# Hybrid retention and stick-breaking encoder: opening sums, idle products and the engine of the norm statistics

## The chip, the cores and the metric

The kernel runs on one core of a Trainium2 chip. The core has a matrix engine (TensorE, PE in the profile), a vector engine (VectorE, DVE), an engine for activation functions (ScalarE, ACT), a general engine (GpSimd, POOL) and a queue that issues DMA transfers (SyncE, SP). Each engine works off its own instructions in order; semaphores tie the engines together. What counts is the device time of one execution in microseconds (us).

## What is computed

Two layers over a sequence of 1024 frames of 1024 features, in float32. Each layer is one mixer with two head groups:

```python
shift, scale, gate = split(silu(c) @ w_ada + b_ada, 3)
h = rms_norm(x, norm_g) * (1 + scale) + shift
rq, rk, rv, rg, sq, sk, sv, sg = split(h @ w_in)
y_ret = group_norm(retention(rot(rq), rot(rk), rv)) * silu(rg)   # 4 heads x 128
y_sb = stick_breaking(sq, sk, sv) * silu(sg)                     # 8 heads x 64
x = x + gate * (concat(y_ret, y_sb) @ w_out)

def group_norm(o):   # at the end of retention()
    mu = mean(o, -1); var = mean((o - mu) ** 2, -1)
    return (o - mu) * rsqrt(var + 1e-6)
```

A final RMSNorm follows. `shift` and `scale` of the first layer are products of one vector, silu(c), with a 1024 x 2048 part of `w_ada`.

## The kernel before

**Tiling.** Frames and features both come in 8 tiles of 128 (t or b for frames, k for features). Each float32 operand of a large product is split into a float16 part and a float16 remainder (`hh`, `hl` for h; `w[:, 0]`, `w[:, 1]` for weights), and a product is made of three: high x high, high x low, low x high. They write results (`acc`) of 128 x 512 to PSUM. PSUM has eight banks: five for general use (`g`), two for the large results (`pj`), one named `av`, which the opening uses under the name `sums`.

**Order.** `Flow` is a planner that runs while the program is built. Every piece of work is a generator; where it says `yield`, it names what it needs. The planner keeps an estimated clock for each engine, prices each instruction (`price`), and takes the ready piece of the lowest rank; `WARM` is the last rank. The order thus found is fixed in the program. A changed price can so change the order anywhere behind it.

**Opening.** `start` issues, for each k, the loads of two 1024 x 128 parts of `w_ada` (scale and shift, tile `ada`, 512 KB each) and one piece of the first weights (`wst`, split into `w`). Four x tiles come first, four more between k = 1 and k = 2; each x tile is normalised, then transposed on TensorE in two halves (`turned`: 32 transposes each, PSUM tile `xt`) and copied to `xT` (`kept`). With `shift` and `scale` for k known, `kept` makes h: `h32` on GpSimd, `hh` on ScalarE, `hl` on VectorE.

The modulation is a sum over 1024 products for each of 128 columns. Before, for k below 4, `first_direct` makes it on TensorE: 8 products with one result column for scale and 8 for shift, both in float32. For k from 4 on, `first_scale` multiplies and adds on VectorE (8 operations over 128 columns in two running sums and an addition) and `first_shift` multiplies on ScalarE (8) and adds on GpSimd (7); then one product with a column of ones (`first_columns`) adds over the partitions. `summed` reads the column out of the bank `sums` on VectorE. The parts for k = 1, 2, 5 and 6 live in a ring of two buffers: that of k = 5 reuses that of k = 1, and that of k = 6 that of k = 2.

`stick_project` for pair 0 of layer 0 starts while h comes in: `begin` takes all 8 k for four results of the first half, and another `begin` (`later`) for three of the second half. Then the attention of that pair starts with products called `z`.

`awake` fills TensorE with idle products (a constant tile by itself, 256 columns) wherever nothing else is ready, until h for the first half and k = 0 is done.

**Retention.** `retain` treats one block of 128 frames of one head; there are 2 x 4 x 8 = 64. Its result `po` (128 x 128, PSUM, a bank of `g`) goes through `bn_stats` and `bn_aggr` on VectorE (mean and variance), two small operations on GpSimd (variance plus a constant, power -0.5), then `y0` on VectorE, and `yt` on ScalarE and VectorE. The bank goes free when `y0` has been read from it.

Of the kernel before, what the change touches and what calls it, by code (L numbers as in the profile page):

```python
# [13 lines left out]
F32 = mybir.dt.float32  # L14
AF = mybir.ActivationFunctionType
ALU = mybir.AluOpType
# [22 lines left out]
def retention_constants():  # L39
    f = np.float32  # L40
    lg = np.log1p(-(f(2.0) ** (f(-5.0) - np.arange(4, dtype=f)))).astype(f)
    i = np.arange(P, dtype=f)
    m, c = i[:, None], i[None, :]
    same = (i[:, None] // 64) == (i[None, :] // 64)
    later = (c // 64) > (m // 64)
    mask = np.zeros((P, 4, P), f)
    qdec = np.exp((i[:, None] + f(1.0)) * lg[None, :]).astype(np.float64)
    for h in range(4):
        dec = np.exp((np.abs(c - m) - (c + 1)).astype(np.float64) * lg[h])
        mask[:, h] = np.where(same | later, dec * np.exp((m - 127.0) * lg[h]), 0.0) * RS  # L50
    kdec = np.exp((f(127.0) - i)[:, None] * lg[None, :]).astype(f)
    bdec = [float(np.exp(f(P) * lg[h])) for h in range(4)]


    cols = np.concatenate([kdec * f(DS * VS), EPS * P * (VS * RS / qdec) ** 2], 1).astype(f)
    return mask, cols, bdec
# [43 lines left out]
class Flow:  # L100
# [32 lines left out]
    def price(self, kind, name, outs, ins):  # L133
# [12 lines left out]
        if kind == "act":  # L146
            scales = sum(1 for a in ins[1:] if a.free_size() == 1)
            return n / 1.2 + (51 if ins[0].space == PSUM else 93) + 93 * scales
# [144 lines left out]
def trunk(ctx: ExitStack, tc, x, c, norm_g, w_ada, b_ada, w_in, w_out, final_g,  # L293
# [195 lines left out]
    def first_scale(ks, scale):  # L489

        yield (), roomt.has()
        roomt.n -= 1
        two = f2("acc").rearrange("p (a f) -> p a f", a=2)[:, :, 0:len(ks) * P]
        for r in range(NK):
            yield [scale], None, "dve"
            acc = two[:, r % 2]
            if r < 2:
                dve.tensor_scalar(acc, scale[:, r], c_act[:, r:r + 1], None, op0=ALU.mult)
            else:
                dve.scalar_tensor_tensor(out=acc, in0=scale[:, r], scalar=c_act[:, r:r + 1], in1=acc,  # L500
                                         op0=ALU.mult, op1=ALU.add)
        acc = two[:, 0]
        dve.tensor_add(acc, acc, two[:, 1])
        yield [acc]
        yield from first_columns(acc, ks, 1)
        roomt.n += 1
# [460 lines left out]
    def retain(l, h, b, acc, state, turn, mask):  # L967
# [17 lines left out]
        dve.scalar_tensor_tensor(out=gs, in0=acc[:, 384:512], scalar=DS, in1=gs,  # L985
# [19 lines left out]

        old, old16 = state[0] or (None, None)
        if b < NT - 1:
# [18 lines left out]
            state[0] = new, new16  # L1026
        yield [("qkT", l, h, b)], roomg.has(), "pe"
# [15 lines left out]
        if b > 0:  # L1043
# [3 lines left out]
        st = wk.tile([P, 6], F32, tag="rbs", name="rbs")  # L1047
        dve.bn_stats(out=st, in_=po[:, 0:P])
        mv = wk.tile([P, 2], F32, tag="rmv", name="rmv")
        dve.bn_aggr(out=mv, in_=st)  # L1050
        ve = wk.tile([P, 1], F32, tag="rve", name="rve")
        pool.tensor_tensor(out=ve, in0=mv[:, 1:2], in1=rcols_sb[:, 4 + h:5 + h], op=ALU.add)
# [3 lines left out]
        dve.scalar_tensor_tensor(out=y0, in0=po[:, 0:P], scalar=mv[:, 0:1], in1=gs,  # L1056
                                 op0=ALU.subtract, op1=ALU.mult)
# [217 lines left out]
    def start():  # L1275
# [34 lines left out]
        for k in range(NK):  # L1310
# [13 lines left out]
            for i, third in enumerate((1, 0)):  # L1324
# [5 lines left out]
                f = first_direct([k], st, third) if k < 4 else (first_shift, first_scale)[third]([k], st)  # L1330
# [12 lines left out]
    def awake():  # L1343

        idle = bank("idle", "pj", 2)
        while True:
            yield [own]
            if ("h", 0, 0, 0) in flow.done:
                return
            pe.matmul(idle[:, 0:256], own[:, 0:P], own[:, 0:256], start=True, stop=True)  # L1350
# [28 lines left out]
```

## Time and profile before

| | |
|---|---|
| runs of before | 1087.74, 1092.58, 1222.69 us, median 1092.58 |
| profiled execution | 1092.43 us, span 1090.0 us |
| TensorE busy | 1053.6 us (97%) |
| VectorE busy | 879.2 us (81%) |
| ScalarE busy | 550.7 us (51%) |
| GpSimd busy | 247.7 us (23%) |
| read from HBM | 92.32 MB |

The span is the time from the first to the last instruction in the trace; 2.4 us lie outside it. In the rows further down, a row of the windows gives the stretch, its length, the busy time of PE, its weight loads (PEld), DVE, ACT and POOL with the number of instructions, the granted TensorE clock as a share of 2.4 GHz, the busy share of the DMA engines and what they moved in GB/s. A row of the timeline gives start, duration, engine, line, operation, result and operands, shapes, count, and in brackets the idle time before it and what ended it. The line is L90 nearly everywhere, that of the recording helper, so the names of tiles tell the work apart. A row of waits gives who waited for whom: total, times, longest. Float32 products appear as two records each where the result has one column. Matmul records overlap, since they are pipelined; the distance between starts is what one costs.

### The profile page before, as it was taken

To read this page: it belongs to the slowest core of one execution; us is meant where nothing else is said; L and a number is where in the kernel's file an instruction comes from. 1 tells how busy PE (TensorE), PEld (TensorE's weight loads), DVE (VectorE), ACT (ScalarE), POOL (GpSimd) and SP (SyncE) were. 2 spreads that over 40 slices of the span, in tenths; PEclk is the share of its full clock that TensorE was granted. 3 is DMA by queue.
4 is the path that set the end of the run, shared out by engine and by line. 5 is a ranking of instruction groups with operands and counts; after the bars stand their busy time and mean duration, and the time that the engine had idled before them with its cause. 6 is when DMAs were issued, how large, how long until landed. Compare 5 with 4: busy or idle time off the path is not lost. (4 is left out here: it accounts for less than half of the span.)

```text
span 1090.0 us, 18647 instructions
## 1 busy us (share of the span) xinstructions
PE 1053.6 (97%) x6472; PEld 525.4 (48%) x6472; DVE 879.2 (81%) x1673; ACT 550.7 (51%) x1263; POOL 247.7 (23%) x557
## 2 busy tenths in 40 slices
PE   6989999999999999999899999999999999999996
PEld 5834444444455544544445444444454445545443
DVE  2488998899899968999455788976899789999544
ACT  3566556535454455481444555544645555555112
POOL 2382330133014202320100034000133013343002
PEclk8699999999999999999999999999999999999999
DMA  9915756766686746367581565665735473647664
GB/s 291 241 50 137 157 112 150 181 137 162 156 201 150 155 91 143 69 172 180 171 239 61 120 142 104 138 159 120 158 78 139 85 153 71 150 82 175 198 238 144
DMA packets 343901, 159.61 MB, mean 146 GB/s; under 512 B 228032, under 2 KB 319232, under 8 KB 343808
## 3 DMA queue, kind: packets, MB, share of 16 engines
q1 hardware_dynamic: 343808, 158.44, 60.3%
q8 instruction: 50, 0.82, 0.3%
q14 instruction: 43, 0.35, 0.1%
HBM read 92.32 MB, written 11.53 MB: 95 GB/s over the span
## 5 line engine op out<-in xcount | busy, mean ns | idle before, releaser
L90 PE MATMUL acc<-hh,w 128*128 128x512 f16 x1024 | 323.0, 381 | 0.7 <-DVE q L90 0.6
L90 PE MATMUL acc<-w,hh 128*128 128x512 f16 x1024 | 305.0, 379 | 0.0
L90 PEld LDWEIGHTS <-w 128*128 128x128 f16 x1536 | 145.7, 99 | 179.7 <-issue 21.3
L90 PE MATMUL acc<-hl,w 128*128 128x512 f16 x512 | 195.0, 381 | 0.8 <-DVE hl L90 0.8
L90 PE MATMUL acc<-w,hl 128*128 128x512 f16 x512 | 194.0, 379 | 0.0
L90 POOL TENSOR_TENSOR t<-t,t 128x128 f32<-128x128 f32 (+1 forms) x192 | 130.9, 696 | 232.6 <-DVE t L90 196.4
L90 PE MATMUL acc<-w,y 128*128 128x512 f16 (+1 forms) x792 | 170.8, 374 | 3.3 <-ACT y L90 3.1
L90 PEld LDWEIGHTS <-hh 128*128 128x128 f16 x1024 | 92.3, 98 | 96.8 <-issue 10.8
L90 DVE TENSOR_TENSOR_SCAN keep<-keep,own 128x640 f32<-128x640 f32 (+3 forms) x60 | 114.3, 1911 | 18.8 <-ACT keep L90 18.7
L90 PEld LDWEIGHTS <-y 128*128 128x128 f16 x792 | 76.5, 98 | 91.2 <-ACT y L90 3.6
L90 DVE SCALAR_TENSOR_TENSOR w<-wst,w 128x512 f16<-128x512 f32 x160 | 110.8, 714 | 8.2 <-ACT w L90 7.9
L90 ACT ACTIVATE w<-wst 128x512 f16<-128x512 f32 x160 | 96.5, 635 | 15.2 <-DMA wst<-in_w_in_dram 11.9
L90 ACT CAST t<-t 128x256 f16<-128x256 f32 (+1 forms) x128 | 44.3, 352 | 88.5 <-POOL t L90 53.3
L90 ACT CAST keep<-beta 128x640 f16<-128x640 f32 (+3 forms) x60 | 53.0, 885 | 63.5 <-DVE beta L90 63.2
L90 PEld LDWEIGHTS <-hl 128*128 128x128 f16 x512 | 50.1, 98 | 60.4
L90 ACT ACTIVATE keep<-z 128x512 f32<-128x512 f32 (+3 forms) x120 | 63.7, 531 | 20.6 <-PE z L90 20.1
L90 DVE TENSOR_TENSOR keep<-beta,keep 128x640 f16<-128x640 f32 (+3 forms) x60 | 61.2, 1024 | 7.5 <-ACT keep L90 7.5
L90 PE MATMUL z<-k,q 64*128 64x512 f16 (+3 forms) x576 | 64.6, 328 | 1.3 <-ACT beta L90 0.5
L90 ACT ACTIVATE beta<-z 128x512 f32<-128x512 f32 (+4 forms) x120 | 64.3, 536 | 0.0
L90 DVE SCALAR_TENSOR_TENSOR beta<-beta,keep 128x639 f32<-128x639 f32 (+3 forms) x60 | 62.5, 1047 | 0.0
L90 DVE TENSOR_TENSOR t<-acc,turn 128x256 f32<-128x256 f32 x128 | 47.9, 415 | 17.2 <-ACT vd L90 16.2
L90 DVE TENSOR_TENSOR_SCAN both<-both,own 128x128 f32<-128x128 f32 (+3 forms) x64 | 55.1, 869 | 7.2 <-ACT both L90 7.2
(122 smaller groups left out, 1307.4 us busy)
## 6 DMA issues: line engine op xcount, KB each, us to landing
wst<-in_w_in_dram SPq DMA_DIRECT2D x128, 256.0 KB, 3.5
wst<-in_w_ada_dram SPq DMA_DIRECT2D x64, 256.0 KB, 3.1
ada<-in_w_ada_dram SPq DMA_DIRECT2D x16, 512.0 KB, 6.5
wst<-in_w_out_dram SPq DMA_DIRECT2D x32, 256.0 KB, 3.4
x<-xh SPq DMA_DIRECT2D x24, 256.0 KB, 2.6
xt<-in_x_dram SPq DMA_DIRECT2D x8, 512.0 KB, 5.3
turn<-in_rot_dram SPq DMA_DIRECT2D x64, 64.0 KB, 2.3
xt<-x SPq DMA_DIRECT2D x8, 512.0 KB, 4.4
```

The source lines that it names most:

```text
L90: real(*args, **kw)
```

## The change

It has four parts.

1. In the opening, `first_direct` now serves k = 0 and 1 for both parts, and k = 2, 3 and 5 for shift alone. `first_scale` serves k = 2 to 7, and `first_shift` k = 4, 6 and 7.
2. `first_scale` is four VectorE operations on the loaded tile: one multiplication over 1024 columns, with silu(c) spread over 128 columns each, and three additions of 512, 256 and 128 columns.
3. Idle products run until h for the second half and k = 7 is planned, and they write columns 256 to 511 of the bank `sums` instead of a tile of their own in `pj`.
4. In `retain`, the statistics come from ScalarE: one activation copies `po` and gives the negative mean by its accumulator, a second squares `po` minus the mean and gives the sum of squares. The constants are scaled to match, `y0` adds the negative mean, and a mark orders the states of successive blocks. The planner's price for an activation with two results rises by 186 ns.

```diff
     def first_scale(ks, scale):
-        yield (), roomt.has()
-        roomt.n -= 1
-        two = f2("acc").rearrange("p (a f) -> p a f", a=2)[:, :, 0:len(ks) * P]
-        for r in range(NK):
+        yield [scale], None, "dve"
+        dve.tensor_tensor(out=scale, in0=scale, in1=c_act[:, :, None].broadcast_to([P, NK, P]), op=ALU.mult)
+        for n in (4, 2, 1):
             yield [scale], None, "dve"
-            acc = two[:, r % 2]
-            if r < 2:
-                dve.tensor_scalar(acc, scale[:, r], c_act[:, r:r + 1], None, op0=ALU.mult)
-            else:
-                dve.scalar_tensor_tensor(out=acc, in0=scale[:, r], scalar=c_act[:, r:r + 1], in1=acc,
-                                         op0=ALU.mult, op1=ALU.add)
-        acc = two[:, 0]
-        dve.tensor_add(acc, acc, two[:, 1])
-        yield [acc]
-        yield from first_columns(acc, ks, 1)
-        roomt.n += 1
+            dve.tensor_add(scale[:, 0:n], scale[:, 0:n], scale[:, n:2 * n])
+        yield [scale]
+        yield from first_columns(scale[:, 0], ks, 1)
...
+        if b > 0:
+            yield [("state", l, h, b - 1)]
...
         yield [po]
-        st = wk.tile([P, 6], F32, tag="rbs", name="rbs")
-        dve.bn_stats(out=st, in_=po[:, 0:P])
-        mv = wk.tile([P, 2], F32, tag="rmv", name="rmv")
-        dve.bn_aggr(out=mv, in_=st)
+
+        junk = turned[:, P:]
+        nm = wk.tile([P, 1], F32, tag="rmv", name="rmv")
+        act.activation(junk, po[:, 0:P], AF.Identity, scale=-1.0 / P, accum_out=nm)
+        yield [nm]
+        sq = wk.tile([P, 1], F32, tag="rbs", name="rbs")
+        act.activation(junk, po[:, 0:P], AF.Square, bias=nm[:, 0:1], accum_out=sq)
+        yield [sq]
         ve = wk.tile([P, 1], F32, tag="rve", name="rve")
-        pool.tensor_tensor(out=ve, in0=mv[:, 1:2], in1=rcols_sb[:, 4 + h:5 + h], op=ALU.add)
+        pool.tensor_tensor(out=ve, in0=sq, in1=rcols_sb[:, 4 + h:5 + h], op=ALU.add)
...
-                f = first_direct([k], st, third) if k < 4 else (first_shift, first_scale)[third]([k], st)
+                f = first_direct([k], st, third) if k < 2 or (k in (2, 3, 5) and not third) else (first_shift, first_scale)[third]([k], st)
...
-        idle = bank("idle", "pj", 2)
+        idle = sums[:, 256:512]
         while True:
             yield [own]
-            if ("h", 0, 0, 0) in flow.done:
+            if ("h", 0, 1, 7) in flow.done:
                 return
-            pe.matmul(idle[:, 0:256], own[:, 0:P], own[:, 0:256], start=True, stop=True)
+            pe.matmul(idle, own[:, 0:P], own[:, 0:256], start=True, stop=True)
```

Over the whole program TensorE has 62 idle products instead of 39, 56 direct sums instead of 64 and 9 column sums instead of 8. All other products are the same in number.

On TensorE, in the opening, `xt` is the transpose of the second half of x, `sums<-c_act,ada` a direct sum and `acc<-hh,w` a product of `begin`. Before, this is how the sums for k = 3 stand:

```order
L90 LDWEIGHTS w
L90 MATMUL acc<-hh,w 128x512
L90 MATMUL sums<-c_act,ada 128x1 x16
L90 MATMUL xt<-ident,xt 128x128 x32
L90 LDWEIGHTS w
L90 MATMUL acc<-hh,w 128x512
```

Now the place between the first products and the transposes reads so (tile numbers shown; of the idle products `sums<-own`, 13 stand ahead of the direct sums of shift 2 and four behind them; `ada_280` holds the parts for k = 2):

```order
L90 LDWEIGHTS own_76
L90 MATMUL sums_113<-own_76 128x256
L90 MATMUL sums_113<-c_act_100,ada_280 128x1 [waits DMAHW3_49]
L90 MATMUL sums_113<-c_act_100,ada_280 128x1 x7
...
L90 MATMUL sums_113<-own_76 128x256 [waits DVE_49]
L90 LDWEIGHTS w_127 [waits Activation_49]
...
L90 MATMUL xt_477<-ident_71,xt_278 128x128
L90 MATMUL sums_113<-c_act_100,ada_288 128x1 [waits DMAHW6_49]
L90 MATMUL sums_113<-c_act_100,ada_288 128x1 x7
```

The direct sums for k = 3 (`ada_288`, shift alone) moved from ahead of the transposes to behind them, those of scale 2 and 3 are gone from here, and an idle product waits for VectorE.

On VectorE, in the opening, before, the sum for scale 5 and what stands among it (`s` and `sh` are the finished columns):

```order
L90 TENSOR_SCALAR acc<-ada,c_act 128x128
L90 TENSOR_TENSOR s_111<-sums,bg 128x1
L90 TENSOR_TENSOR s_111<-s_111,bg 128x1
L90 TENSOR_SCALAR acc<-ada,c_act 128x128
L90 SCALAR_TENSOR_TENSOR acc<-ada,c_act,acc 128x128 x4
L90 TENSOR_TENSOR sh_109<-sums,bg 128x1
L90 SCALAR_TENSOR_TENSOR acc<-ada,c_act,acc 128x128 x2
L90 TENSOR_TENSOR acc<-acc 128x128
```

Now, the place where scale 2 ends and scales 3 and 4 start:

```order
L90 TENSOR_TENSOR hl<-h_460,hh 128x512
L90 COPY xT<-xt 128x512
L90 SCALAR_TENSOR_TENSOR w<-wst,w 128x512
L90 TENSOR_TENSOR ada<-ada 128x128
L90 SCALAR_TENSOR_TENSOR w<-wst,w 128x512
L90 TENSOR_TENSOR sh_109<-sums,bg 128x1
L90 TENSOR_TENSOR ada<-ada,c_act 128x1024
L90 TENSOR_TENSOR s_111<-sums,bg 128x1
L90 TENSOR_TENSOR s_111<-s_111,bg 128x1
L90 SCALAR_TENSOR_TENSOR w<-wst,w 128x512
L90 TENSOR_TENSOR ada<-ada 128x512
L90 TENSOR_TENSOR ada<-ada,c_act 128x1024
```

The eight operations on 128 columns became one on 1024 and three additions, and the end of scale 2 moved behind the copies of the transposed second half.

## Rows read from the trace of the kernel before

**Rows 1.** Windows: busy time in the two long stretches behind the opening

```profile
120.00:540.00 420.00, 411.00 (x2631) 199.76 (x2630) 371.49 (x707) 218.85 (x514) 90.86 (x217) 1.00 0.65 149
540.00:1000.00 460.00, 455.44 (x2827) 218.63 (x2825) 382.06 (x730) 244.22 (x573) 98.63 (x228) 1.00 0.55 126
```

**Rows 2.** Waits of PE over the whole span, longest first

```profile
PE acc L90 <- ACT y L90: 3.1, 2, 1.6
PE sums L90 <- POOL ada L90: 2.8, 2, 1.5
...
PE acc L90 <- DVE hl L90: 0.8, 1, 0.8
PE sums L90 <- DVE acc L90: 0.7, 1, 0.7
...
PE sums L90 <- DVE sh L90: 0.4, 1, 0.4
```

**Rows 3.** Timeline of PE: the opening, and transposes of layer 1 at 540 us

```profile
9.13 6.89 PE L90 MATMUL idle<-own 128*128 128x256 bf16 x37
...
26.93 3.73 PE L90 MATMUL sums<-c_act,ada 128*128 128x1 f32 x32 [0.41 <-DVE sh L90]
...
34.46 3.96 PE L90 MATMUL sums<-c_act,ada 128*128 128x1 f32 x32
...
40.56 6.82 PE L90 MATMUL sums<-c_act,ada 128*128 128x1 f32 x32
47.24 6.10 PE L90 MATMUL xt<-ident,xt 128*128 128x128 f32 x32
53.18 0.38 PE L90 MATMUL acc<-hh,w 128*128 128x512 f16 x1
...
92.25 0.36 PE L90 MATMUL z<-k,q 64*128 64x128 f16 x6
...
540.19 0.60 PE L90 MATMUL pht<-ident,xt 128*128 128x128 f32 x4
540.62 2.75 PE L90 MATMUL acc<-w,y 128*128 128x512 f16 x12
```

**Rows 4.** Chain that ended last: start, us, what; a stretch of dense products

```profile
1006.91 24.61 PE acc L90 x114
```

**Rows 5.** Windows of the opening: granted clock (third number from the end) and transfers

```profile
26.93:30.50 3.57, 3.57 (x32) 3.57 (x33) 2.86 (x6) 3.15 (x6) 1.98 (x4) 1.00 1.08 287
...
40.56:47.20 6.64, 6.64 (x33) 6.64 (x32) 0.28 (x1) 0.21 (x1) 0.00 (x0) 0.50 1.18 291
47.24:53.10 5.86, 5.86 (x33) 5.86 (x34) 3.29 (x6) 3.78 (x7) 2.66 (x3) 0.58 0.46 130
...
53.18:92.25 39.07, 34.78 (x169) 16.14 (x167) 31.91 (x74) 23.88 (x56) 27.05 (x44) 1.00 0.12 35
```

**Rows 6.** Timeline of ACT: the last normalisation of an x tile

```profile
39.63 1.14 ACT L90 ACTIVATE xt<-xt,rs 128x1024 f32<-128x1024 f32 x1
```

**Rows 7.** Timeline of the DMA queue: the pair of loads for k = 6

```profile
38.69 2.60 SPq L90 DMA_DIRECT2D ada<-in_w_ada_dram  x2
```

**Rows 8.** Groups by line and form: VectorE operations near the new ones

```profile
L90 DVE TENSOR_TENSOR keep<-beta,keep 128x1024 f16<-128x1024 f32 x16 | 19.5, 1216 | 2.5 <-ACT keep L90 2.5
...
L90 DVE TENSOR_TENSOR xh<-xh,up 128x512 f32<-128x512 f32 x24 | 16.6, 692 | 1.6 <-DMA xh<-x 0.9
...
L90 DVE SCALAR_TENSOR_TENSOR acc<-ada,c_act,acc 128x128 f32<-128x128 f32 x24 | 9.9, 465 | 0.0
```

**Rows 9.** Groups by line and form: the statistics on DVE, and nearest ACT rows

```profile
L90 DVE BATCH_NORM_STATS2 rbs<-po 128x6 f32<-128x128 f32 x64 | 18.3, 287 | 3.3 <-PE po L90 3.1
...
L90 DVE BATCH_NORM_AGGREGATE rmv<-rbs 128x2 f32<-128x6 f32 x64 | 11.6, 182 | 2.2
...
L90 ACT ACTIVATE rg<-acc 128x128 f32<-128x128 f32 x64 | 17.6, 275 | 28.6 <-PE acc L90 28.6
...
L90 ACT ACTIVATION_READ_ACCUMULATOR junk<-xt 128x1 f32 x22 | 4.1, 187 | 0.0
```

More of the change, by code (lines that the diff above doesn't have):

```diff
@@ L52, in retention_constants @@
     bdec = [float(np.exp(f(P) * lg[h])) for h in range(4)]
-    cols = np.concatenate([kdec * f(DS * VS), EPS * P * (VS * RS / qdec) ** 2], 1).astype(f)
+    cols = np.concatenate([kdec * f(DS * VS), EPS * P * P * (VS * RS / qdec) ** 2], 1).astype(f)
     return mask, cols, bdec
@@ L147, in price @@
             scales = sum(1 for a in ins[1:] if a.free_size() == 1)
-            return n / 1.2 + (51 if ins[0].space == PSUM else 93) + 93 * scales
+            read = 186 * (len(outs) > 1)
+            return n / 1.2 + (51 if ins[0].space == PSUM else 93) + 93 * scales + read
         if kind == "dve":
@@ L984, in retain @@
                                  op0=ALU.mult, op1=ALU.subtract)
-        dve.scalar_tensor_tensor(out=gs, in0=acc[:, 384:512], scalar=DS, in1=gs,
+        dve.scalar_tensor_tensor(out=gs, in0=acc[:, 384:512], scalar=DS * P ** 0.5, in1=gs,
                                  op0=ALU.mult, op1=ALU.mult)
@@ L1026, in retain @@
             state[0] = new, new16
+            flow.mark(("state", l, h, b))
         yield [("qkT", l, h, b)], roomg.has(), "pe"
@@ L1055, in retain @@
         y0 = sm
-        dve.scalar_tensor_tensor(out=y0, in0=po[:, 0:P], scalar=mv[:, 0:1], in1=gs,
-                                 op0=ALU.subtract, op1=ALU.mult)
+        dve.scalar_tensor_tensor(out=y0, in0=po[:, 0:P], scalar=nm[:, 0:1], in1=gs,
+                                 op0=ALU.add, op1=ALU.mult)
         roomg.n += 1
```

## The prediction

> **What bounds the kernel now.** I read the windows of busy time first. Behind the opening TensorE hardly rests: 411.0 of 420 us between 120 and 540 us, 455.4 of 460 between 540 and 1000 [rows 1]. So past the opening an edit is worth at most the 13.6 us of rest in the first two windows, and only where a wait of TensorE hangs on it. The longest of those waits are for `y` from ScalarE, 3.1 us in two pieces [rows 2].
>
> The opening is different: TensorE is "busy" there with work that is small or of no use. The timeline [rows 3] shows, in order: 37 idle products, direct sums of the modulation (16 for each k, 32 records), at 47.24 us the 32 transposes of the second half of x, and from 53.18 us the product stream of `begin`. That stream is the first work of any size: 8 k x 7 results x 3 = 168 products of 512 columns. The program's order puts 12 ahead of the sums for k = 2 and 6 behind them, so 150 remain at 53.18 us. One costs 24.61 / 114 = 0.216 us [rows 4], so 150 cost 32.4 us; TensorE waits 2.8 + 0.8 + 0.7 = 4.3 us for modulation and `hl` [rows 2]; that leaves, of the 39.1 us to the first product for `z` at 92.25 us [rows 3], 2.4 us for eight column sums: 0.3 each.
>
> The reader should look at one place above all: the sums for k = 3 fill 40.56 to 47.24 us, 6.82 us for a job that took 3.73 us at 26.93 us. The granted clock tells why: 1.00 in the early stretch, 0.50 in the late one, that is the lower level of 1.2 GHz, not the upper of 2.4 [rows 5]. The transposes queue behind them, although their last input was normalised at 39.63 + 1.14 = 40.8 us [rows 6], and run at a mean of 0.58 themselves [rows 5]. Everything after 92 us is a full TensorE, so a microsecond won before it should arrive at the end.
>
> **The opening, step by step.** The order of TensorE is common to both kernels up to 34.46 us (one idle product fewer). From there the changed order has 13 idle products, the 8 sums of shift 2, 4 idle products, 3 products for k = 1, then the transposes. Idle products cost 6.89 / 37 = 0.186 us with the clock up [rows 3]; 13 cost 2.4 us, twice that at the lower level. I take 2.9, because the clock was low just before and I expect it to rise during them. Eight sums are half of 3.73 or half of 6.82 us: 1.9 to 3.4, and I take 1.9, since idle products stand ahead. Four idle products are 0.7 us, and the last of them waits for VectorE, which reads a sum from the same bank: 0.4 us, by the one such wait of before, for `sh` [rows 2]. Three products are 0.65. So the transposes can start at 34.46 + 2.9 + 1.9 + 1.1 + 0.65 = 41.0 us. Their input is there: in ScalarE's order the last normalisation, which ended at 40.8 us [rows 6], no longer stands behind the `hh` of k = 2 and its wait for a sum.
>
> The transposes take 5.9 us at the lower level (47.24 to 53.18); at full clock four take 0.43 us (540.19 to 540.62 [rows 3]), so 32 take 3.5. I take 5.0, because two engines that also have `hl` and `hh` to make copy the results out of three banks. The dense stream then starts at 46.0 us instead of 53.18. Bounds: everything at the upper level, 43.7; everything at the lower, 50.9.
>
> Behind it TensorE has more to do than before: 153 products (33.0 us), 16 direct sums that were moved behind the transposes (shift 3 and shift 5, 3.7 us), nine column sums at 0.3 us (2.7), seven idle products (1.3). That is 40.7 us. Of the 4.3 us of waits I leave 1.0. The sums of VectorE are shorter: for one k, eight operations at about 0.47 us and an addition, some 4.2 us, become one pass of 1024 (1.22 us, by the nearest row) and additions of 512, 256 and 128 (0.69, then 0.42 and 0.30 as an estimate on the line through these two rows): 2.6 us [rows 8]. In 53 to 92 us VectorE was busy 31.9 us, GpSimd 27.1, ScalarE 23.9 [rows 5]. With 5 scales of 2.6 for 4 of 4.2 VectorE has 28, and GpSimd loses the seven additions of shift 5. All fit under 40.7 us of TensorE work, which is the cover; without it the chain of sum, `h` and `hl` shows again, with 4.3 us as before. So `z` begins at 46.0 + 40.7 + 1.0 = 87.7 us, **4.6 us earlier**. By the bounds: 43.7 + 40.7 + 0 = 84.4 (7.9 earlier) and 50.9 + 40.7 + 4.3 = 95.9 (3.6 later).
>
> **A transfer that gets later.** The pair for k = 6 reuses the buffer of k = 2. Before, it was issued at 38.69 us [rows 7]; now it must wait for the column sum of scale 2, which the new order puts six products and eight sums behind the transposes, at about 46.0 + 1.9 + 1.3 = 49.2 us. Behind it in SP's queue stand a weight piece, the pair for k = 7 and another piece: 2.5 MB, about 9 us at 291 GB/s [rows 5], so to some 59 us. The products for k = 7 are the last 21 before `z`, from about 87.7 - 21 x 0.216 = 83.2 us, and the chain from landing to them (2.6 us of sums, `h`, `hl`) is a few us. I charge nothing; it would cost only if the pair slipped by some 15 us more.
>
> **The norm statistics.** On VectorE two operations of 0.287 and 0.182 us go, 64 times: 30.0 us [rows 9]. On ScalarE two activations and two reads of the accumulator come, 2 x (0.275 + 0.187) = 0.92 us [rows 9], 59 us in all, on an engine that was busy 218.9 of 420 and 244.2 of 460 us [rows 1]; the second activation waits for the first's sum, with the sigmoids of the attention queued behind it and VectorE's scans behind those. The chain from `po` to the statistics is 0.45 us longer. In no row of before does TensorE wait for these statistics [rows 2]; what hides them is the products of other heads. A relieved VectorE can shorten the 3.1 us of `y`, a fuller ScalarE can lengthen them. Bounds: 3 us gained, or 64 x 0.45 = 29 us lost if every block passed its delay on through a bank that `po` holds. I take 0.5 gained.
>
> **Sum.** 1092.43 (the profiled execution, span 1090.0; the median of 1092.58 is next to it) - 4.6 - 0.5 = 1087.3, say **1087**.
>
> One rule speaks against the idle products. The wait on TensorE for VectorE's read of a sum is 0.4 us, once [rows 2]. The Trainium skill, "PSUM — Partial Sum Buffer", section "PSUM bank collisions raise a hardware error", says that two engines must not touch one bank in the same partitions at once, even at different columns, so it is to be guarded bank by bank; the idle products now share the bank of the sums. By it each of the three groups of idle products behind 34 us waits for a read, 1.2 us at the row's price in place of the 0.4 in the sum: 1088.1 instead of 1087.3. No row of before has idle products in that bank, so none can say which.
>
> **Rivals.** (a) *The clock stays up.* If the idle products hold the upper level through sums and transposes, the early bounds hold: 7.9 us from the opening, and with the 3.1 us of `y` waits 1092.4 - 11.0 = **1081**. For it: the clock was 1.00 right after the first transposes; against: it was 0.50 through 6.6 us of sums [rows 5], and sums remain. The Trainium skill, "TensorE: Matmul & The Clock Gate", Part 1, says that the throttled level is the default and activity releases it; by that rule this case would be the likely one, and the trace agrees in the direction alone. (b) *The gain is lost again*, because the transposes start no earlier (copies, a low clock) or because the order behind 92 us, newly made by the planner, has 5 us more of waits beside its 13.6: **1092**. For it: the planner's order behind 92 us differs in many places. Against: TensorE's work there is the same, piece for piece. (c) *ScalarE becomes the bound of the retention chain.* `po` holds one of five banks until VectorE has the mean, and the mean now waits in ScalarE's queue behind sigmoids. If half the 64 blocks pass 0.45 us on, that is +14: 1092.4 - 4.6 + 14 = **1102**; it decides from about 12 blocks on (12 x 0.45 = 5.4, more than the 5.1 gained). Against: ScalarE is idle half the time.
>
> **How the numbers follow.** My forecast (1084 to 1091) 0.50, (a) 0.17, (b) 0.20, (c) 0.13. From 1080 to 1095 holds the forecast, (b) and most of (a): the range. Faster by over 2% would need 1070.7, beyond every bound but a sum of all: 0.01. Slower by over 2% (above 1114; 2% is about what a measurement here can tell from no change) needs (c) at nearly full price: 0.04. The rest, 0.95, is no difference.
>
> **What would show it.** Right: transposes at 40 to 42 us, stream from about 46, `z` at 86 to 89; nearly no waits between; a thinner stretch of DMA around 43 to 49 us; the clock not at 0.50 for 12 us on end. Wrong: transposes at 45 or later; `z` past 91; TensorE waiting for `po`'s banks or ScalarE; more than 17 us of rest between 120 and 1000 us.

## The result and the profile after

The changed kernel takes 1101.93 us (median; 1097.51 to 1106.59), the kernel before 1089.32 in the same comparison. The ratio is 1.0120, 95% interval [1.0091, 1.0150]: 1.2% slower, outside the predicted 1080 to 1095. The profiled execution took 1106.59 us with a span of 1104.8. The run of before at 1222.69 us counts in its median, but is left out of the ratio as a slow run.

The engine busy times moved as the diff says: VectorE 851.1 us (879.2 before), ScalarE 591.6 (550.7), GpSimd 281.7 (247.7). TensorE is busy 1056.0 of 1104.8 us, 2.4 us more than before.

The timeline of TensorE in the opening answers [rows 3]: columns are start, duration, engine, line, operation, operands, shapes, count, and the idle time ahead with what ended it.

```profile
37.32 2.92 PE L90 MATMUL xt<-ident,xt 128*128 128x128 f32 x24
40.93 1.21 PE L90 MATMUL xt<-ident,xt 128*128 128x128 f32 x8 [0.69 <-ACT xT L90]
41.98 2.15 PE L90 MATMUL sums<-c_act,ada 128*128 128x1 f32 x16
43.98 0.59 PE L90 MATMUL acc<-hh,w 128*128 128x512 f16 x1
...
77.62 1.01 PE L90 MATMUL sums<-ones,ada 128*128 128x1 f32 x4 [2.27 <-DVE ada L90]
...
92.46 0.45 PE L90 MATMUL z<-k,q 64*128 64x128 f16 x7
```

The transposes start 10 us earlier than the 47.24 us of before and the dense stream 9 us earlier than 53.18; yet the first product for `z` comes at 92.46 us, where before had 92.25. The nine microseconds are gone by 92 us. How many of the nine were the program's own is taken up further down, with a second execution of each kernel. Here is the window from the dense stream to `z`, to be held against the last of [rows 5], in which before was busy for 34.78 of 39.07 us:

```profile
43.98:92.46 48.48, 44.51 (x196) 20.98 (x197) 35.23 (x63) 23.11 (x48) 30.61 (x39) 0.87 0.35 90
```

TensorE idles 4.0 us there, no more than the 4.3 of before, but it is busy 9.7 us longer. One part of this is the work that the change moves behind the transposes, by the forecast's count 40.7 us for 34.8. The other part is the clock. These are windows of after (granted clock third from the end):

```profile
44.00:46.00 2.00, 2.00 (x6) 0.70 (x7) 1.35 (x3) 1.27 (x4) 1.38 (x2) 0.50 0.04 8
...
58.00:60.00 2.00, 2.00 (x6) 0.76 (x5) 1.41 (x3) 2.00 (x8) 1.92 (x3) 0.50 0.97 273
...
78.00:84.00 6.00, 6.00 (x17) 2.42 (x17) 2.20 (x6) 2.04 (x3) 2.20 (x8) 0.50 0.00 0
```

These ten microseconds ran at 1.2 GHz; at the upper level the same work would have taken about 5 us less, as an estimate. SP's queue, which answers [rows 7], and ScalarE's timeline show what else is late:

```profile
46.95 1.26 SPq L90 DMA_DIRECT2D ada<-in_w_ada_dram  x2
48.29 1.25 SPq L90 DMA_DIRECT2D wst<-in_w_in_dram  x1
```

```profile
56.07 0.63 ACT L90 ACTIVATE w<-wst 128x512 f16<-128x512 f32 x1 [5.81 <-DMA wst<-in_w_in_dram]
```

The pair for k = 6 is issued at 46.95 us (before: 38.69), and the weight piece behind it at 48.29. ScalarE, in its order, waits 5.81 us for that piece; the `hh` of k = 3 and the products of the next shift sums stand behind the wait. Since TensorE's own idle time is no longer than before, this wait is not shown to cost it anything.

The larger loss is behind `z`. From the first product for `z` to the end of the span I call *the remainder*: 1104.8 - 92.46 = 1012.3 us, against 1090.0 - 92.25 = 997.8 before, **14.6 us more**. The windows that answer [rows 1], from `z` on (length, then TensorE's busy time), and the row that sums them:

```profile
92.46:540.00 447.54, 433.31 (x2751) 208.58 (x2750) 375.65 (x688) 254.41 (x684) 110.45 (x224) 1.00 0.68 150
540.00:1000.00 460.00, 450.52 (x2787) 216.32 (x2786) 363.47 (x655) 261.67 (x676) 105.13 (x220) 1.00 0.55 123
1000.00:1104.80 104.80, 94.61 (x525) 46.95 (x522) 55.74 (x86) 27.74 (x70) 20.92 (x34) 0.98 0.66 187
sum 1012.34, PE 978.43 PEld 471.85 DVE 794.87 ACT 543.82 POOL 236.50; mean PE 326.14 PEld 157.28 DVE 264.95 ACT 181.27 POOL 78.83
```

The same three windows of before sum to this:

```profile
sum 997.75, PE 974.92 PEld 471.08 DVE 829.07 ACT 502.29 POOL 205.52; mean PE 324.98 PEld 157.03 DVE 276.36 ACT 167.43 POOL 68.51
```

TensorE idles 1012.34 - 978.43 = 33.9 us in after and 22.8 in before. So 11.1 of the 14.6 us are new idle time and 3.5 are longer busy time, which was not traced. The waits of TensorE behind `z` (total, times, longest), beside [rows 2], name the first new one. The first row is from after, the second from before:

```profile
PE psc L90 <- POOL t L90: 9.4, 10, 2.1
```

```profile
PE psc L90 <- POOL t L90: 1.3, 5, 0.5
```

`psc`, the first product of a retention block, waits 9.4 us for the rotated tile `t` from GpSimd; before, that wait was 1.3 us. On GpSimd stand the two small operations behind the statistics, `rve` and `rrs`. In the groups by form (total, mean ns of one) they last 0.50 and 0.96 us, where before had 0.190 and 0.652 (after first, then before):

```profile
L90 POOL TENSOR_TENSOR rrs<-rve,nhalf 128x1 f32<-128x1 f32 x64 | 61.3, 958 | 5.0
...
L90 POOL TENSOR_TENSOR rve<-rbs,rcols_sb 128x1 f32<-128x1 f32 x64 | 31.7, 495 | 91.2 <-ACT t L90 91.1
```

```profile
L90 POOL TENSOR_TENSOR rrs<-rve,nhalf 128x1 f32<-128x1 f32 x64 | 41.7, 652 | 5.0
...
L90 POOL TENSOR_TENSOR rve<-rmv,rcols_sb 128x1 f32<-128x1 f32 x64 | 12.1, 190 | 123.2 <-DVE rmv L90 119.5 <-ACT keep L90 3.6
```

The prices that [rows 8] and [rows 9] stood for came out as follows: the scale of one k takes 1.306 + 0.724 + 0.527 + 0.584 = 3.14 us, not 2.6; the statistics take 0.280 + 0.205 + 0.372 + 0.203 = 1.06 us a block on ScalarE, not 0.92. The additions of the scale sums are not dearer by themselves. At their shortest the three take 0.68, 0.42 and 0.28 us, as forecast. Of the six over 128 columns, the first had no GpSimd operation beside it and took 0.28 us; the other five had one, and took 0.47 to 0.77 us. Here are the mean, the first and the last of them:

```profile
L90 DVE TENSOR_TENSOR ada<-ada 128x128 f32<-128x128 f32 x6 | 3.5, 584 | 0.0
```

```profile
43.15 0.28 DVE L90 TENSOR_TENSOR ada<-ada 128x128 f32<-128x128 f32 x1
...
76.80 0.77 DVE L90 TENSOR_TENSOR ada<-ada 128x128 f32<-128x128 f32 x1
```

### The profile page after: what moved, and what is told of

Read it like the earlier page. It is cut to its first block, busy times and chain, and to the rows that moved or that the text cites. A ratio compares the mean times of both kernels' runs of the same rounds, so it can differ in the third digit from the quotient of the medians.

```text
span 1104.8 us, 18789 instructions
## 1 busy us (share of the span) xinstructions
PE 1056.0 (96%) x6481; PEld 520.6 (47%) x6481; DVE 851.1 (77%) x1533; ACT 591.6 (54%) x1511; POOL 281.7 (26%) x550
## 4 chain that ended last, share of the span: by engine, by line
PE 37%; DVE 6%; issue 4%; POOL 4%; DMA 2%; ACT 2%; SPq 2%; POOLq 0%; DVEq 0%; ACTq 0%
PE acc L90 31%; PE z L90 2%; PE av L90 2%; SPq L90 2%; POOL t L90 1%; DMA xt<-x 1%; DVE t L90 1%; POOL rrs L90 1%; DVE keep L90 1%; PE po L90 1%; DVE beta L90 1%; POOL rve L90 1%; PE psc L90 1%; DVE w L90 1%; DVE h L90 1%
## 5 line engine op out<-in xcount | busy, mean ns | idle before, releaser
L90 PE MATMUL acc<-hh,w 128*128 128x512 f16 x1024 | 327.2, 386 | 1.4 <-DVE q L90 1.2
L90 PE MATMUL acc<-hl,w 128*128 128x512 f16 x512 | 197.7, 386 | 0.0
L90 POOL TENSOR_TENSOR t<-t,t 128x128 f32<-128x128 f32 (+1 forms) x192 | 123.3, 656 | 280.4 <-DVE t L90 233.5
L90 ACT ACTIVATE keep<-z 128x512 f32<-128x512 f32 (+3 forms) x120 | 63.5, 529 | 14.6 <-PE z L90 14.0
L90 POOL TENSOR_TENSOR rrs<-rve,nhalf 128x1 f32<-128x1 f32 x64 | 61.3, 958 | 5.0
```

Source lines behind the costliest of these rows:

```text
L90: real(*args, **kw)
```

## The experiments

The questions were which part makes the remainder longer, whether the parts work by themselves or through the planner's order, and what the opening really gained. All figures stand in one table; the edits and what they showed follow. "Remainder" is span minus start of `z`, of the profiled execution; "idle t" is TensorE's wait for `t` from GpSimd behind `z`; the pair is the mean of `rve` and `rrs` in ns.

| kernel | `z` at | remainder | idle t | pair | time, us | ratio to before |
|---|---|---|---|---|---|---|
| before | 92.25 | 997.8 | 1.3 | 190, 652 | 1089.3 | |
| before again (g4) | 86.33 | 997.4 | 1.6 | 192, 652 | 1085.87 (one run) | |
| changed | 92.46 | 1012.3 | 9.4 | 495, 958 | 1101.93 | 1.0120 [1.0091, 1.0150] |
| changed again (f4) | 88.54 | 1012.2 | 9.9 | 500, 967 | 1102.5 (one run) | |
| e1 opening alone | 87.10 | 1005.4 | 3.2 | 189, 648 | 1098.11 | 1.0114 [1.0057, 1.0171] |
| e2 statistics alone | 87.99 | 1006.4 | 8.5 | 455, 914 | 1096.42 | 1.0079 [1.0051, 1.0107] |
| e3 idle products alone | 88.63 | 1006.1 | 2.3 | 197, 670 | 1096.91 | 1.0080 [1.0048, 1.0111] |
| e4 before, planner's margin 410 | 96.20 | 1004.1 | 1.9 | 203, 672 | 1096.82 | 1.0060 [1.0028, 1.0093] |
| f2 before, margin 390 | 87.56 | 1007.7 | 4.6 | 189, 646 | 1100.94 | 1.0095 [1.0064, 1.0126] |
| f1 statistics on ScalarE, order of before | 86.19 | 1001.6 | 2.8 | 293, 736 | 1097.33 | 1.0052 [1.0018, 1.0086] |
| f3 changed, margin 410 | 91.36 | 1008.8 | 8.9 | 553, 906 | 1102.76 | 1.0112 [1.0055, 1.0170] |
| g1 statistics on VectorE, changed order | 88.76 | 1012.4 | 7.5 | 456, 859 | 1103.62 | 1.0149 [1.0090, 1.0208] |
| g2 changed, GpSimd priced as measured | 91.31 | 1007.2 | 5.7 | 467, 837 | 1100.31 | 1.0109 [1.0063, 1.0154] |
| g3 changed, scale 2 on TensorE | 94.79 | 1008.2 | 9.2 | 488, 775 | 1103.87 | 1.0149 [1.0101, 1.0197] |
| h1 as g1, `y0` moved up | 91.74 | 1025.6 | 9.4 | 262, 914 | 1118.31 | 1.0265 [1.0227, 1.0303] |

**Each part alone, and the planner alone (e1 to e4).** The variants of before also carry the mark on the states of successive blocks (the `yield [("state", ...)]` and `flow.mark` of the diff); alone, it leaves the order of every engine as it was, as f1 further down shows, which carries it too. e1 has parts 1, 2 and 3 of the change (`first_scale`, the line that chooses between the three kinds of sum, and the idle products), e2 part 4 with its price of 186 ns; their edits stand in the diff ahead. e3 has part 3 alone, and e4 none of them; no run has parts 1 and 2 without part 3:

```diff
# e3
-        idle = bank("idle", "pj", 2)
+        idle = sums[:, 256:512]
-            if ("h", 0, 0, 0) in flow.done:
+            if ("h", 0, 1, 7) in flow.done:
-            pe.matmul(idle[:, 0:256], own[:, 0:P], own[:, 0:256], start=True, stop=True)
+            pe.matmul(idle, own[:, 0:P], own[:, 0:256], start=True, stop=True)
# e4
-SLACK = 400
+SLACK = 410
```

`SLACK` is the margin in ns that the planner adds when TensorE must wait for another engine. It is in no instruction; it only makes another order.

> The changed kernel with the norm statistics put back on VectorE (bn_stats, bn_aggr); the opening's edits and the mark on the states stay. In the trace of the changed kernel the first product for z starts at 92.5 us against 92.25 before, and the 12 us are lost behind it. Theory A (the statistics on ScalarE cost the 12 us, the opening nothing): within 3 us of before, z at 91 to 94 us. Rival B (any new order of the planner behind the opening costs this): 1096 to 1103, as changed. Rival C (the opening costs it, by leaving work late for what follows): 1099 or more.

> The kernel before with only the statistics moved to ScalarE (and the planner's price of 186 ns for it). Theory A: 1099 to 1103, 10 to 13 us above before; GpSimd's two small operations behind the statistics take 0.4 us or more and 0.8 us or more in the mean instead of 0.19 and 0.65, and TensorE waits 6 us or more for the rotated t. Rival C: 1087 to 1091. Rival B: anything between 1085 and 1103, with no tie to the waits for t.

> The kernel before with only the idle products changed: longer, and in the bank of the sums. If the idle products alone keep the clock up and let the transposes start earlier, z at 88 to 91 us and 1085 to 1088. If the sums for k = 3 still stand in front of the transposes, nothing changes: z at 91 to 93 us, within 2 us of before. Rival B: a new order, up to 10 us above before.

> The kernel before with one constant of the planner changed (SLACK 410 instead of 400 ns): the same instructions in another order on every engine from about the first z on. Theory A: within 3 us of before. Rival B (the order alone moves the time by as much as the change did): 5 us or more away from before, either side.

All four are slower, and their remainders lie between 1004.1 and 1006.4 us. e1, e3 and e4 came out as rival B has it. e2 has the long pair and the waits for `t` of theory A (8.5 us), but takes 1096.4 us, less than its 1099 to 1103. The one that changes nothing but the planner's margin loses 6.3 us behind `z`, where those with real parts lose 7.6 to 8.6. So a part's price can't be read from a kernel in which the planner has ordered everything anew.

**The order held or varied (f1 to f4).** f1 takes before with its order held: the planner is told of `bn_stats` and `bn_aggr`, and the program gets the two activations at that place. f2 is before with a margin of 390 and f3 the changed kernel with one of 410, each by the one line shown for e4; f4 is the changed kernel once more.

```diff
# f1
-        dve.bn_stats(out=st, in_=po[:, 0:P])
-        dve.bn_aggr(out=mv, in_=st)
+        act.real.activation(junk, po[:, 0:P], AF.Identity, scale=-1.0 / P, accum_out=nm)
+        act.real.activation(junk, po[:, 0:P], AF.Square, bias=nm, accum_out=sq)
+        flow.note("dve", "bn_stats", [st], [po[:, 0:P]])
+        flow.note("dve", "bn_aggr", [mv], [st])
```

> The kernel before with the statistics on ScalarE, but with the planner told that they are still bn_stats and bn_aggr on VectorE: TensorE, GpSimd and the DMA queue keep the order of before instruction by instruction. If moving the statistics itself costs (the GpSimd pair behind them gets slower and the rotated t comes late): 1095 to 1100, with the pair above 0.4 and 0.8 us in the mean and the rest of the program behind z 5 us or more longer than the 997.8 us of before. If only the new order cost (theory B): 1086 to 1091, the rest of the program 996 to 1000 us.

> The kernel before with the planner's constant SLACK at 390 instead of 400 ns, a second order without any other edit. If the order of before is one of the good ones among many (theory B): 1092 to 1100, the rest behind z 1002 to 1008 us, as in the run with 410. If 410 was a bad draw: within 3 us of before.

> The changed kernel with SLACK at 410: the same edits, another order. Theory B alone: the rest behind z falls to 1003 to 1008 us, where the other orders of the kernel before lie. If the statistics on ScalarE cost on top of it: 1008 to 1014 again, with 6 us or more of waits of TensorE for t.

> The changed kernel once more, for a second trace of its opening. In the run with the opening's edits alone z began at 87.1 us, in the changed kernel's first trace at 92.5 after a wait of 2.3 us and a fall of the clock to 0.50 around 80 us. If that was the draw of one execution: z at 86 to 90 us here. If it belongs to the program: 91 to 94.

In f1's trace every engine has the order of before, apart from the exchanged operations. In that order ScalarE's statistics cost 1001.6 - 997.8 = 3.8 us in the remainder; that, and the pair at 293 and 736 ns, lies between the two cases expected. The margin of 390 costs 9.9 us, with nothing changed in the work. Here are the sums of the windows behind `z` for the two orders of before that are new by the margin alone, 410 (e4) and 390 (f2):

```profile
sum 1004.10, PE 975.97 PEld 473.06 DVE 825.42 ACT 500.78 POOL 199.70; mean PE 325.32 PEld 157.69 DVE 275.14 ACT 166.93 POOL 66.57
```

```profile
sum 1007.74, PE 979.00 PEld 472.82 DVE 829.08 ACT 501.54 POOL 207.55; mean PE 326.33 PEld 157.61 DVE 276.36 ACT 167.18 POOL 69.18
```

They lose in other places than the changed kernel. In e4 the longest waits are those for DMA transposes, 6.7 us at `psc` and 3.7 at `av`, where before has 4.0 and 0.5. f4 repeats the changed kernel's remainder to 0.2 us while its `z` starts 3.9 us earlier: the remainder belongs to the program, the opening varies between executions. f3 shortens the remainder by 3.5 us by the margin alone; its waits for `t` stay at 8.9 us.

**The converse, and three repairs (g1 to g4).** g1 keeps the order of the changed kernel and takes the statistics on VectorE again, so it is f1 the other way round. g2 tells the planner what the small GpSimd operations really take. g3 lets scale 2 be a direct sum, so that its buffer comes free early. g4 is before once more.

```diff
# g1, each operation at the place where its counterpart stood
-        act.activation(junk, po[:, 0:P], AF.Identity, scale=-1.0 / P, accum_out=nm)
+        dve.real.bn_stats(out=st, in_=po[:, 0:P])
+        dve.real.bn_aggr(out=mv, in_=st)
+        flow.note("act", "activation", [junk, nm], [po[:, 0:P], nm])
-        act.activation(junk, po[:, 0:P], AF.Square, bias=nm[:, 0:1], accum_out=sq)
+        flow.note("act", "activation", [junk, sq], [po[:, 0:P], nm[:, 0:1], sq])
# g2
-                return 500 if outs[0].tensor.name.startswith(("rrs", "rs", "r_")) else 268
+                return (960 if outs[0].tensor.name.startswith("rrs") else 500) if outs[0].tensor.name.startswith(("rrs", "rve", "rs", "r_")) else 268
# g3, in the line that chooses the kind of sum
-if k < 2 or (k in (2, 3, 5) and not third)
+if k < 3 or (k in (3, 5) and not third)
```

> The changed kernel with the order of all its remaining instructions held, but the statistics of the 64 retention blocks taken on VectorE again (two batch-norm operations in place of two activations and their two accumulator reads, at the same place of the order). It is the reverse of the run that put the statistics on ScalarE in the order of before. Counted is the part behind the first product for z (before 997.8 us with 13.5 us of listed TensorE waits; changed 1012.3 with 24.9). Theory: of the 14.5 us about two thirds belong to the planner's new order and a third to the statistics; then this part takes 1006 to 1010 us with 17 to 21 us of waits, the two small GpSimd operations fall back towards 0.2 and 0.65 us, and the time is about 1096 to 1099. Rival one, the statistics alone do it: 998 to 1001 us, 13 to 15 us of waits, time about 1089. Rival two, the order alone does it: 1011 to 1013 us, 23 to 25 us of waits, time about 1102.

> The changed kernel with one number of the planner changed: it prices the two small GpSimd operations behind the statistics at 0.50 and 0.96 us, as the changed trace has them, instead of 0.27 and 0.50. It computes the same. If the late rotated tiles t (9.4 us of TensorE's waits in the changed kernel, 1.3 before) come from these operations taking longer than the planner counts with, the new order keeps clear of them: waits for t under 4 us, the part behind the first z at 1004 to 1008 us instead of 1012.3, time 1094 to 1099. Rival: the pair is late whatever the planner thinks, or any new order costs about the same: waits for t still 5 to 10 us, that part 1008 to 1014, time 1098 to 1104.

> The changed kernel with scale 2 summed on TensorE again (8 direct sums), so that the buffer of k = 2 comes free early, as before. Theory on the opening: in the changed kernel the pair of loads for k = 6 is issued at 46.95 us instead of 38.69, and ScalarE, in its order, then waits 5.81 us for the weight piece behind it; here the pair goes out at 38 to 42 us, that wait of ScalarE is under 1.5 us, TensorE waits under 2 us for modulation between the transposes and z (3.9 in the changed kernel), and z starts 2 to 4 us earlier than 92.5 in an execution with the clock alike: 86 to 90. Rival: the late pair was covered and only the clock decides: z at 88 to 93 with the same waits. The order behind z is a new one: by the theory on orders 1005 to 1012 us behind z; time 1094 to 1101.

> The kernel before, unchanged, for a second profile of it: its first product for z (92.25 us in the first) and the part behind (997.8). If the part behind z is a property of the order and only the opening varies between executions, that part is 997 to 999 us again, while z falls anywhere from 85 to 93. Rival: the part behind z varies too by several us, and then differences of 4 us between kernels there mean nothing: outside 995 to 1001.

g1 decides the main question, for rival two. With the statistics back on VectorE, and all else in the changed order, the three windows behind `z` sum to the same figure as in the changed kernel, and the pair stays long (456 and 859 ns in the table):

```profile
sum 1012.44, PE 978.14 PEld 470.90 DVE 818.05 ACT 499.06 POOL 229.76; mean PE 326.05 PEld 156.97 DVE 272.68 ACT 166.35 POOL 76.59
```

So here the 14.6 us lie in the order of the instructions. Which engine makes the statistics is worth 0.1 us in this order, and 3.8 us in that of before. g4 gives the remainder of before as 997.4 us, which makes differences of 4 us there meaningful.

g2 came to the remainder that was expected (1007.2 us), but its waits for `t` fell to 5.7 us and not below 4, and the pair is nearly as long. As most other new orders land between 1004 and 1009 too, its 5 us don't show that the price was the cause. g3 missed. The pair for k = 6 is issued at 39.94 us and ScalarE's wait for the weight piece is gone, as expected; but `z` is at 94.79 us, and TensorE still idles 4.5 us between stream and `z`. The new order puts 12 products where the changed one has three, and 24 direct sums where it has 8, ahead of the transposes, which start at 46.98 us as in before; the clock was at 0.50 through those 12 products (39.8 to 44.8 us), so this one execution does not tell how much of the delay is the order's.

**What lies beside the pair (h1).** In before, `y0` follows `bn_aggr` on VectorE at once. Here is one block of before on VectorE and on GpSimd:

```profile
245.83 0.18 DVE L90 BATCH_NORM_AGGREGATE rmv<-rbs 128x2 f32<-128x6 f32 x1
246.05 0.35 DVE L90 SCALAR_TENSOR_TENSOR t<-po,rmv,rg 128x128 f32<-128x128 f32 x1
```

```profile
246.09 0.19 POOL L90 TENSOR_TENSOR rve<-rmv,rcols_sb 128x1 f32<-128x1 f32 x1 [3.37 <-DVE rmv L90]
246.36 0.55 POOL L90 TENSOR_TENSOR rrs<-rve,nhalf 128x1 f32<-128x1 f32 x1
```

And one of after, VectorE and then GpSimd:

```profile
279.11 0.74 DVE L90 SCALAR_TENSOR_TENSOR acc<-wst,c_act,acc 128x512 f32<-128x512 f32 x1
279.77 0.95 DVE L90 SCALAR_TENSOR_TENSOR beta<-beta,keep 128x767 f32<-128x767 f32 x1
280.64 0.34 DVE L90 SCALAR_TENSOR_TENSOR t<-po,rmv,rg 128x128 f32<-128x128 f32 x1
280.90 1.28 DVE L90 SCALAR_TENSOR_TENSOR w<-wst,w 128x512 f16<-128x512 f32 x2
```

```profile
279.39 1.38 POOL L90 TENSOR_TENSOR rve<-rbs,rcols_sb 128x1 f32<-128x1 f32 x1 [6.23 <-ACT t L90]
280.85 1.74 POOL L90 TENSOR_TENSOR rrs<-rve,nhalf 128x1 f32<-128x1 f32 x1
```

`rve` takes 0.19 us beside `y0` (the tile `t<-po`), which reads one operand from PSUM. It takes 1.38 us beside `acc` and `beta`, which read two from SBUF, and ends when `beta` does. `rrs` likewise ends some 0.4 us behind the two `w` operations. Counted over the timeline, 11 of the 128 operations of the pair last over 0.1 us longer than the shortest of their kind in before, 35 in f1, 60 in g1 and 72 in after. All 72 have a VectorE operation beside them that, by the names of its tiles, reads two operands from SBUF; of the 56 short ones 24 have none. In before at least 60 of the 64 `rve` have none, and all 64 are short. The Trainium skill, "SBUF — State Buffer", section "🔬 SBUF: two separate sides", says that GpSimd shares a pair of ports with VectorE, and that one of the two blocks for a whole instruction when VectorE reads two operands from SBUF. These rows agree.

h1 moves `y0` in g1 back to where before has it, ahead of one to seven others in 58 of the 64 blocks, and nothing else on any engine:

```diff
         dve.real.bn_aggr(out=mv, in_=st)
+        y0 = sm
+        dve.real.scalar_tensor_tensor(out=y0, in0=po[:, 0:P], scalar=mv[:, 0:1], in1=gs,
+                                      op0=ALU.subtract, op1=ALU.mult)
...
-        y0 = sm
-        dve.real.scalar_tensor_tensor(out=y0, in0=po[:, 0:P], scalar=mv[:, 0:1], in1=gs,
-                                      op0=ALU.subtract, op1=ALU.mult)
```

> The kernel with the changed order and the statistics on VectorE, with one operation moved: y0, which reads po from PSUM, stands on VectorE directly behind the second statistics operation, as it does in the kernel before, and not two or three operations later. All other engines have the same rows in the same order. In the trace of before the two small GpSimd operations run beside y0 and take 0.19 and 0.65 us; in the changed order they run beside VectorE operations on two operands in SBUF, end with these, and take 0.46 and 0.86 us, and TensorE then waits 7.5 us for the rotated tile t behind them. Theory: what lies beside them on VectorE is the cause; then they take about 0.2 and 0.65 us again, the waits for t fall from 7.5 to 2 to 4.5 us, and the part behind the first product for z falls from 1012.4 to 1006 to 1010 us, time 1097 to 1101. Rival one: the pair gets short but t stays late for another reason: waits for t 6 to 8 us, that part 1011 to 1013 us, time about 1103. Rival two: the pair stays long (its length has nothing to do with VectorE).

The groups by form on GpSimd and the sum of the three windows behind `z`, both of h1:

```profile
L90 POOL TENSOR_TENSOR rrs<-rve,nhalf 128x1 f32<-128x1 f32 x64 | 58.5, 914 | 5.0
L1058 POOL TENSOR_TENSOR rve<-mv,rcols_sb 128x1 f32<-128x1 f32 x64 | 16.8, 262 | 95.7 <-DVE mv L1048 88.9 <-ACT k L90 6.6
```

```profile
sum 1025.56, PE 983.88 PEld 472.40 DVE 825.18 ACT 497.61 POOL 222.81; mean PE 327.96 PEld 157.47 DVE 275.06 ACT 165.87 POOL 74.27
```

`rve` got short (0.262 us), as the theory has it; `rrs` did not, since `y0` is over before it; and the waits for `t` rose to 9.4 us. The remainder grew by 1025.56 - 1012.44 = 13.1 us, which none of the theories had: 7.4 of idle time on TensorE and 5.7 of longer busy time. An operation of 0.35 us, moved ahead of one to seven others in 58 blocks, costs 0.2 us a block, and h1 takes 2.65% longer than before. No single wait of TensorE explains it, the largest rises being 1.9 us each, for `t` and for its DMA transpose. What the operations that `y0` overtakes hold up was not traced further. So the long pair is real, but it is not shown to be what makes the changed order slow.

## Why the prediction was wrong

**"Against: TensorE's work there is the same, piece for piece."** This is the step that failed. It was the reason to take the 13.6 us of rest between 120 and 1000 us [rows 1] as given, and to put the order's risk (rival b) at 5 us with a chance of 0.20. The work is the same, but the waits belong to the order; rival (b) had this mechanism, at half its size. Between 120 and 1000 us TensorE now rests 880 - 406.4 - 450.5 = 23.1 us, past the 17 us that the prediction named as a sign of being wrong. Two orders of before that differ in nothing but the planner's margin cost 6.3 and 9.9 us; every new order that was run has a remainder of 1004 us or more, where before has 997 to 998. Those planned with the statistics on VectorE (e1, e3, e4, f2) have 1005.8 on the mean, those with ScalarE (e2, f3, changed, g2, g3) 1008.6, but the two groups overlap. The order of before is better than each of the nine new ones, and whatever made the planner start afresh here began with a loss of 6 us or more. Why it is good stays open, and so does what in the changed order holds TensorE up.

**"I take 0.5 gained" for the statistics.** No gain appeared in either order: 3.8 us lost in the order of before, nothing in the changed one. Rival (c) had nearly the right time, 1102, by luck: with ScalarE freed of the statistics (g1), nothing came back in the changed order.

**"`z` begins at 87.7 us, 4.6 us earlier."** Two errors stand in this. The first is the start of the subtraction: the 92.25 us came from one execution, in which the sums for k = 3 ran at 0.50. In g4, the same program, they don't:

```profile
38.08 3.83 PE L90 MATMUL sums<-c_act,ada 128*128 128x1 f32 x32
41.76 5.51 PE L90 MATMUL xt<-ident,xt 128*128 128x128 f32 x32
47.11 0.38 PE L90 MATMUL acc<-hh,w 128*128 128x512 f16 x1
...
86.33 0.36 PE L90 MATMUL z<-k,q 64*128 64x128 f16 x6
```

Of the 6.82 us at "the place to look at above all", 3 were not the program's. The transposes of after, at 37.3 us, also look better than they are against the 41.0 forecast, since 2.2 us of that come from the stretch which both orders share (it ends at 32.30 us there, at 34.46 in before). f4 and g4 end this stretch at the same time, 31.82 and 31.83 us, and so compare the two openings. The transposes and the stream of f4:

```profile
36.44 2.92 PE L90 MATMUL xt<-ident,xt 128*128 128x128 f32 x24
...
42.80 0.38 PE L90 MATMUL acc<-hh,w 128*128 128x512 f16 x1
```

From the same point the transposes start 41.76 - 36.44 = 5.3 us earlier and the stream 4.3 us earlier, where 7.2 were forecast; yet `z` comes 2.2 us later. The windows from stream to `z`, of f4 and of g4, give the second error:

```profile
42.80:88.54 45.74, 40.07 (x196) 19.37 (x196) 35.23 (x63) 23.51 (x49) 30.58 (x39) 0.96 0.36 96
```

```profile
47.11:86.33 39.22, 34.77 (x168) 16.14 (x166) 32.04 (x75) 24.16 (x57) 27.09 (x44) 1.00 0.21 57
```

The work behind the stream is 5.3 us more in f4, much as forecast. But the idle time is 5.7 us for 4.5, where the prediction had "of the 4.3 us of waits I leave 1.0". That is the term that was mis-sized: the shorter sums on VectorE did not end the waits, of which the longest, 2.27 us, is for a scale sum. The bounds for the stream, 43.7 and 50.9, come to 44.0 and 51.8 by the prediction's own prices; nothing hangs on it.

In the quicker executions before reaches `z` at 86.3 (g4) and 86.2 us (f1, whose opening is that of before), the changed order at 88.5 (f4) and 88.8 (g1): some 2.4 us later. In the slower ones it is 92.25 against 92.46. Taking the remainders from the medians of the times instead leaves the changed opening about 1.5 us ahead. Either way the opening won nothing like 4.6 us.

**"A transfer that gets later: I charge nothing."** The pair was issued at 46.95 us, near the 49.2 expected. The prediction had followed the transfer only to the products of its own k, and missed the weight piece behind it in SP's queue and the engine that waits for it: ScalarE's order holds the `hh` of k = 3 and the shift products behind that piece, for 5.81 us. But no run shows that TensorE paid for it. In g3 this wait is gone, and TensorE's idle time between stream and `z` is 4.5 us, no less than the 4.0 of the changed kernel's first execution.

**Right** were the move of the transposes, the place and the direction of the late transfer, the 40.7 us of work from the stream to `z` (40.1 us busy in f4, of which some 1.7, as an estimate, were lost to the lower clock between 76 and 80 us), and that the change stays within 2%. Of the price that the rule on the bank puts on the idle products, little appeared: behind 30 us one of them waits for a read, for 0.25 us.

## What to carry over

When a planner makes the order, compare first with an order that is new but changes nothing: here a margin of 410 or 390 in place of 400 ns cost 6 and 10 us, where the whole change cost 14.6 behind `z` and the statistics by themselves 0.1 to 3.8. To price an edit, hold the order and exchange the instructions in place, in both orders if they differ. And take a stage's time from more than one execution before you count what a change will win in it.

## What was not expected of the hardware

The same program reaches `z` at 92.25 or 86.33 us, by the clock granted in its opening (0.50 from 18 to 24 us and from 40 to 52 us in the first; 1.00 from 18 to 24 us and above 0.50 for most of the later stretch in the second); the part behind differs by 0.4 us. In after, the clock read 0.50 from 78 to 84 us, right behind a wait of TensorE of 2.27 us; in g1, with the same wait at the same place, it stayed at 1.00, so the wait alone does not decide it.

Two GpSimd operations on one column, 0.18 and 0.55 us at their shortest, last up to 1.64 and 2.62 us in after beside VectorE operations on two SBUF operands. The same pair of engines shows it the other way round: the VectorE addition over 128 columns, 0.28 us at its shortest, lasts up to 0.77 us beside GpSimd operations, and its mean (0.584) is longer than that of the addition over 256 columns (0.527). No run moved these additions, so GpSimd as the cause is not shown.
